# Sums of x split before the norms' copy, and the value projections' weight sums by adding DMAs, in a hybrid decoder trunk

## The chip, the cores and the metric

The kernel runs on one core of a Trainium2 chip. The metric is the device time of one execution in microseconds. The kernel before takes 791.1 us, the median of three runs (790.81 to 793.31). The engines are named as the profile names them: PE is TensorE (matmuls), PEld its loads of the stationary operand, DVE is VectorE, ACT ScalarE, POOL GpSimd, SP SyncE, which issues most DMAs. Each engine executes its own instructions in the order of the program and waits at an instruction until the semaphores it names are there.

## The reference

One layer of a decoder trunk for one sequence of 512 tokens, D = 1024, with 16 learned meta tokens in front (528 rows), all float32:

```python
u = rms_norm(h, norm_gain)                       # h: 16 meta rows, then x
proj = u @ w_in                                  # one combined projection, cut into
(rq, rk, rv, rg, gq, gk, gv, gg, glr, m_ret, m_gla) = jnp.split(proj, points, axis=-1)
o_ret = retention(rope(rq), rope(rk), rv)        # 4 heads: keys of 256, values of 512
o_ret = head_group_norm(o_ret) * silu(rg)
log_a = log_sigmoid(glr @ w_gate_up + b_gate) / 16
o_gla = gated_linear_attention(gq, gk, gv, log_a)  # 4 heads: keys of 128, values of 256
o_gla = head_rms_norm(o_gla) * silu(gg)
merged = sigmoid(m_ret) * (o_ret @ w_branch_ret) + sigmoid(m_gla) * (o_gla @ w_branch_gla)
out = rms_norm(h + merged @ w_out, final_norm_gain)[meta rows dropped]
```

## The kernel before, in words

PE works in fp32r. A float32 operand is split into a high part (a cast on ACT, `_h`) and a low part (a subtraction on DVE, `_l`), both at line 153, and a product takes three matmuls (high by high, high by low, low by high). A weight block of 128 partitions x 1024 elements (512 rows by 256 columns of w_in) is loaded raw by SP's queue into one of six buffers, and split into one of three buffers for each part.

The projections through w_in are done in groups of a 512-row by 512-column piece with two halves of tokens, two of columns and two of the depth (`quad`). A group is not done as eight products of blocks but as seven, in the manner of Strassen and Winograd: sums of x's blocks (S1 to S4, split once for the whole kernel into `fh`/`fl`) meet sums of weight blocks. The seven products come in the order 1, 2, 6, 7, 5, 4, 3, each 24 matmuls of 128x256 into one of the PSUM banks b, a, c. Product 1 takes the block w11, product 2 w21, product 6 w11 + x3 (added on DVE into w11), product 7 the sum x3, product 5 the sum x1, product 4 w21 + the new w11 (DVE), product 3 w22. The sums x3 and x1 come in one of two ways. With `adds` true, SP loads one block and POOL issues a second DMA that adds the other block to it in memory. With `adds` false, four blocks are loaded and DVE makes the two sums (lines 315 and 316). Before each product its weights are split, so ACT and DVE work one or two products ahead of PE. Results leave PSUM by copies (`_x`) and additions (`vs`, and its split vh, vl).

The groups come in this order: gv0, gq0 and gk0 (plain projections, `proj_a`), gg0, gqk1, gv1, gg1; then for each retention head h the group rqk, then rg, the gates mg or mr and the branch projection br of an earlier head, and rv; at the end the output projection wo. "Value groups" here are gv1 and rv0 to rv3; rv groups come directly before the next head's rqk.

The 16 meta tokens would make a poor moving operand, so their rows for keys and values are made by 32-column matmuls on the unsplit weights (`um` stationary, line 306), four row groups into one PSUM bank (`psm`, in the trace rv_pm or rqk_pm); the bank is then split (rvm_h, rvm_l) and its row groups are summed by two matmuls with a selection matrix (rvm_s, lines 446 and 447). In a value group before, the sixteen such matmuls are done ahead of product 1 from w11, w21, w12, w22; the split and the summing are deferred by a list, `late`, which is run out after product 5 (and after product 1).

The scheduler inside the framework places instructions by their dependences; the dense matmuls are pinned in the order of the program (`pin`, `order`), and `act` and `vec` chain instructions of the first part on ACT and DVE. `weave` steps a dense generator and a second chain of work in turn, and calls `tick` between steps.

At the start, x is loaded, its blocks' sums are made (u00, u01, u10, u11), gv0 runs on the plain blocks, the norms' reciprocal root is spread over the columns (PE's rb, copied to SBUF by ACT), and gq0 and gk0 follow; woven into them are the GLA forget gates (z, Abs, Exp and a correction at lines 654 to 664) and `sums()`, the split of the four sums of x, which gg0 is the first group to need.

Of the kernel before, what the change touches and what calls it, by code (L numbers as in the profile page):

```python
# [20 lines left out]
F32 = mybir.dt.float32  # L21
# [6 lines left out]
P = 128  # L28
D = 1024
T = 512  # L30
NM = 16
# [76 lines left out]
def hybrid_kernel(ctx: ExitStack, tc: tile.TileContext, I, out: bass.AP):  # L108
# [30 lines left out]
    rb = cp.tile([P, 2, HT], F32, name="rb")  # L139
    um = cp.tile([P, KD, 32], F32, name="um")  # L140
    sel = cp.tile([P, P], F32R, name="sel")
# [54 lines left out]
    def rstd_of(x, n, rows, name, eps=EPS):  # L196
        v = sp.tile([P, 1], F32, tag="rv", name=f"{name}_v")
        r = sp.tile([P, 1], F32, tag="rr", name=f"{name}_r")
        nc.vector.tensor_scalar(v[:rows], x, 1.0 / n, eps, op0=ALU.mult, op1=ALU.add)
        nc.gpsimd.tensor_tensor(r[:rows], v[:rows], mhalf[:rows], op=ALU.pow)  # L200
        return r
# [29 lines left out]
    def tick():  # L231

        pend[:] = [(n - 1, f) for n, f in pend]
        while pend and pend[0][0] <= 0:
            pend.pop(0)[1]()

    late = []
# [12 lines left out]

    def quad(cols, rows, name, evac, meta=None, adds=True):

# [25 lines left out]
        def product(i, form, w, ps, fresh):  # L278
            hi, lo = wsplit([P, 4, 256], f"{name}_{i}")
            split(hi, lo, w)  # L280
            for t in range(2):
                col = slice(t * P, (t + 1) * P)
                for kk in range(4):
                    u = [f[form][:, kk, col] if rows else f[form][:, kk, :256] for f in (fh, fl)]
                    v = [f[:, kk, :] if rows else f[:, kk, col] for f in (hi, lo)]
                    first = fresh and kk == t == 0
                    for j, (x1, x2) in enumerate(((0, 0), (0, 1), (1, 0))):
                        l, r = (u[x1], v[x2]) if rows else (v[x1], u[x2])
                        m = nc.tensor.matmul(ps[:, t, :], l, r, start=first and j == 0, stop=kk == 3 and j == 2,  # L289
                                             skip_group_check=not fresh or t == 1)  # L290
                        if t == kk == j == 0:
                            pin(m)
            order[:] = [m]
# [7 lines left out]
        if meta is not None:  # L301
            psm = (ppt if adds else pat)(f"{name}_pm")
            for n in range(1 if adds else 2):
                for kh in range(2):
                    for g in range(4):
                        nc.tensor.matmul(psm[32 * g:32 * g + 32, n * 256:(n + 1) * 256], um[:, 4 * kh + g, :],
                                         (w11, w21)[kh][:, g, :] if n == 0 else (w12, w22)[kh][:, g, :], start=n == 0 and kh == 0, stop=kh == 1,
                                         skip_group_check=n > 0)
        product(1, A11, w11, b, True)
# [16 lines left out]
        x = copy(c, 3)  # L326
        if meta is not None:
            late.append(lambda: meta(psm))
        yield
        product(5, S1, x1, b, False)  # L330
# [3 lines left out]
        product(4, A22, w21, c, False)  # L334
        evac(0, 1, c, y)
        yield
        product(3, S4, w22, b, False)
# [220 lines left out]
    for kh in range(2):  # L558
        for k in range(4):
            x = nc.scalar.activation(u[kh][:, k], u[kh][:, k], AF.Copy, scale=ng[:, 4 * kh + k:4 * kh + k + 1])  # L560
            if kh == 1:
                act(x)
        x = nc.vector.tensor_copy(um[:, 4 * kh:4 * kh + 4, :NM].rearrange("p k (h m) -> p k h m", h=2),
                                  u[kh][:, :, :, 256:HT])
        if kh == 1:
            vec(x)
    u00, u01, u10, u11 = u[0][:, :, 0], u[1][:, :, 0], u[0][:, :, 1], u[1][:, :, 1]
    vec(nc.vector.tensor_sub(u11, u11, u10))
# [42 lines left out]
    leave(2)  # L611
    leave(3)
    act(nc.scalar.copy(rb[:, :, :256], rbm.rearrange("p (h t) -> p h t", h=2)))
    act(nc.scalar.copy(rb[:, :, 256:], rbp[:, HT:HT + NM].rearrange("p (h m) -> p h m", h=2)))
    h, l = split(*parts["gq0", 1], loaded.pop(("gq0", 1)))
    act(h)
    vec(l)

    def sums():
        for i, x in ((S2, u00), (S3, u10), (S1, u11), (S4, u01)):  # L620
            h, l = split(fh[i][:, :, :HT], fl[i][:, :, :HT], x)
            after(h, ends["act"])
            after(l, ends["vec"])
            yield

# [69 lines left out]
    def gla_v(p):  # L695
        yield from quad((C_GV + p * 512, C_GV + p * 512 + 256), True, f"gv{p}", rows_into(gv[p]),
                        lambda psm: meta_v(psm, p), False)

# [5 lines left out]
    def gla_qk(p):  # L704
# [26 lines left out]
        if p:  # L731
            yield from quad((C_GK + p * 256, C_GQ + p * 256), False, f"gqk{p}", evac, meta)
            return
# [189 lines left out]
    next(gates)  # L923
    weave(gla_qk(0), turns(sums(), gates))
    for i in range(4):
# [42 lines left out]
    def ret_qk(h):  # L968

        q = rp.tile([P, 2, 2, 256], F32, tag="ql", name=f"q{h}")  # L970
        k = rp.tile([P, 2, 2, HT], F32, tag="kl", name=f"k{h}")
        R["raw", h] = q, k

        def evac(n, th, x, y):
            total(q[:, :, th] if n else k[:, :, th, :256], x, y)

        def meta(psm):
            nc.scalar.copy(k[:, :, :, 256:], meta_columns(psm, f"rkm{h}"))

        yield from quad((C_RK + h * 256, C_RQ + h * 256), False, f"rqk{h}", evac, meta)  # L980

# [24 lines left out]
    def ret_v(h):  # L1006
# [23 lines left out]

        yield from quad((C_RV + h * 512, C_RV + h * 512 + 256), True, f"rv{h}", evac, meta, False)

# [32 lines left out]
    def ret_attention(h):  # L1065
# [7 lines left out]
        def values(ib):  # L1073
            ps = pat(f"av{h}{ib}")
            for jb in range(ib + 1):
                o = SOFF[jb] + (ib - jb) * P
                mm3(ps, sh[:, o:o + P], sl[:, o:o + P], vh[:, jb, :], vl[:, jb, :], jb == 0, False)
            nc.tensor.matmul(ps, sm[:, ib * P:(ib + 1) * P], vm, start=False, stop=True)
            b6 = sp.tile([P, 6], F32, tag="b6", name=f"b6{h}{ib}")
            mv = sp.tile([P, 2], F32, tag="mv", name=f"mv{h}{ib}")  # L1080
            nc.vector.bn_stats(b6, ps)
            nc.vector.bn_aggr(mv, b6)
            r = rstd_of(mv[:, 1:2], 1.0, P, f"g{h}{ib}")
            nm = sp.tile([P, 1], F32, tag="nm", name=f"nm{h}{ib}")
            nc.vector.scalar_tensor_tensor(nm, mv[:, 0:1], -1.0, r, op0=ALU.mult, op1=ALU.mult)  # L1085
            on = tmp(f"on{h}{ib}")
            nc.scalar.activation(on, ps, AF.Identity, scale=r, bias=nm)  # L1087
            nc.vector.tensor_mul(sg[:, ib, :], on, sg[:, ib, :])
# [104 lines left out]
    def evac_out(half):  # L1193
        def f(t, ps, o=0, n=512):
# [10 lines left out]
            if half == 0 or o + n < 512:  # L1205
                return
            r = sp.tile([P, 1], F32, tag="rr", name=f"fr{t}")
            nc.gpsimd.tensor_tensor(r, v, mhalf, op=ALU.pow)
# [58 lines left out]
```

## Time and profile before

| what | value |
|---|---|
| median of three runs | 791.1 us (790.81 to 793.31) |
| the profiled execution | 791.0 us, its span 789.2 us |
| PE busy | 771.3 us, 98% of the span, 5407 matmuls |
| DVE, ACT, POOL busy | 570.7, 449.5, 139.8 us |
| DMA | 117.91 MB, HBM read 99.20 MB |

A row of a timeline reads: start in us, duration, engine, line, operation, output<-input, shapes, how many; in brackets, if the engine was idle before, how long and whose work ended that. In a table of windows each engine has its busy time and count, and after them come PE's granted clock, the share of the DMA engines and GB/s. The instructions of a group bear the names of their buffers without the number that tells them apart, so that `rv_h` is the high part of any product of any rv group.

### The profile page before, as it was taken

The page shows a single profiled execution, that of the slowest core. Times are in us where ns is not written, and L with a number is a line of the kernel's source. Part 1 is how long each engine was busy: PE and PEld are TensorE (multiplying, and loading weights), DVE is VectorE, ACT ScalarE, POOL GpSimd, SP SyncE. Part 2 cuts the span into 40 slices and gives each one's busy share as a digit, 9 for nine tenths or more (in the row PEclk, how much of TensorE's full clock was granted, in tenths as well). Part 3 has the DMA queues.
Part 4 walks back from the last instruction along what each step waited for, and adds up shares of the span by engine and source line. Part 5 has one row for each costly group of instructions (what it writes and reads, how often), then busy time and mean ns, then how long its engine had stood idle before and what let it go on. Part 6 is the DMA issues. An engine that isn't in the chain of part 4 may idle for free.

```text
span 789.2 us, 13635 instructions
## 1 busy us (share of the span) xinstructions
PE 771.3 (98%) x5407; PEld 699.3 (89%) x5407; DVE 570.7 (72%) x824; ACT 449.5 (57%) x743; POOL 139.8 (18%) x200
## 2 busy tenths in 40 slices
PE   8999999999999999999999999999999899999996
PEld 5788989999889899989989999989999898888785
DVE  5588688677654579778967687977686988576832
ACT  7697775677654456546646545645455655363422
POOL 2110220101312313100320100340111101333031
PEclk9999999999999999999999999999999999999999
DMA  9871703642148983833684562695475327799202
GB/s 284 261 185 39 171 12 98 150 144 81 67 129 207 242 185 108 187 107 108 183 240 137 112 156 108 161 246 131 123 153 122 108 81 215 121 306 304 94 2 106
DMA packets 94601, 117.91 MB, mean 149 GB/s; under 512 B 5957, under 2 KB 80581, under 8 KB 94281
## 3 DMA queue, kind: packets, MB, share of 16 engines
q1 hardware_dynamic: 74600, 85.58, 35.7%
q0 software_dynamic: 19936, 31.46, 20.5%
q8 instruction: 42, 0.69, 0.4%
q14 instruction: 23, 0.18, 0.1%
HBM read 99.20 MB, written 17.83 MB: 148 GB/s over the span
## 4 chain that ended last, share of the span: by engine, by line
PE 79%; DVE 8%; ACT 4%; DMA 4%; issue 3%; POOL 1%; POOLq 0%; SPq 0%; DVEq 0%; ACTq 0%
PE rv_b L289 6%; PE rg_b L289 5%; PE rqk_b L289 4%; PE mg_b L289 3%; PE rg_c L289 3%; PE br_p L192 3%; PE br_p L191 3%; PE br_p L188 3%; PE rv_c L289 2%; PE gg_b L289 2%; PE rqk_c L289 2%; PE bg_p L192 2%; PE bg_p L191 2%; PE bg_p L188 2%; PE wo_p L188 2%
## 5 line engine op out<-in xcount | busy, mean ns | idle before, releaser
L192 PE MATMUL br_p<-oh,br_l 128*128 128x512 f32 x128 | 50.6, 395 | 0.0
L191 PE MATMUL br_p<-ol,br_h 128*128 128x512 f32 x128 | 50.5, 395 | 0.0
L188 PE MATMUL br_p<-oh,br_h 128*128 128x512 f32 x128 | 50.5, 395 | 0.0
L153 ACT CAST rv_h<-rv_w 128x1024 fp32r<-128x1024 f32 x24 | 25.3, 1052 | 28.2 <-DVE rv_w L318 10.2
L1087 ACT ACTIVATE on<-av,nm,g_r 128x512 f32<-128x512 f32 x16 | 12.5, 778 | 48.7 <-DVE nm L1085 48.6
L885 POOL DMA_DIRECT2D kept<-mt x24 | 19.8, 825 | 109.7 <-ACT mt L1147 109.5
L153 DVE TENSOR_TENSOR rv_l<-rv_w,rv_h 128x1024 fp32r<-128x1024 f32 x24 | 29.3, 1222 | 8.8 <-ACT rv_h L153 8.8
L153 DVE TENSOR_TENSOR rg_l<-rg_w,rg_h 128x1024 fp32r<-128x1024 f32 x20 | 24.4, 1221 | 7.9 <-ACT rg_h L153 7.9
L192 PEld LDWEIGHTS br_p<-oh,br_l 128*128 128x128 f32 x128 | 24.0, 187 | 5.8
L191 PEld LDWEIGHTS br_p<-ol,br_h 128*128 128x128 f32 x128 | 24.0, 188 | 5.2
L188 PEld LDWEIGHTS br_p<-oh,br_h 128*128 128x128 f32 x128 | 24.0, 188 | 5.1
L153 DVE TENSOR_TENSOR rqk_l<-rqk_w,rqk_h 128x1024 fp32r<-128x1024 f32 x20 | 24.4, 1221 | 5.3 <-ACT rqk_h L153 5.3
L269 POOL DMA_DIRECT2D rqk_x<-in_w_in_dram x8 | 10.4, 1306 | 98.2 <-DVE vl L153 50.3
L188 PE MATMUL wo_p<-wo_h,mh 128*128 128x512 f32 (+1 forms) x72 | 26.6, 370 | 0.7 <-DVE mt L1152 0.7
L289 PE MATMUL rg_b<-rg_l,fh 128*128 128x256 f32 x96 | 27.0, 282 | 0.3 <-DVE rg_l L153 0.3
L153 ACT CAST rg_h<-rg_w 128x1024 fp32r<-128x1024 f32 x20 | 21.0, 1052 | 11.0 <-PE br_p L191 5.0
L289 PE MATMUL rqk_b<-fh,rqk_h 128*128 128x256 f32 x96 | 27.2, 284 | 0.0
L289 PE MATMUL rqk_b<-fh,rqk_l 128*128 128x256 f32 x96 | 27.1, 283 | 0.1
L289 PE MATMUL rqk_b<-fl,rqk_h 128*128 128x256 f32 x96 | 27.0, 282 | 0.0
L289 PE MATMUL rv_b<-rv_h,fl 128*128 128x256 f32 x96 | 27.0, 281 | 0.0
L289 PE MATMUL rv_b<-rv_l,fh 128*128 128x256 f32 x96 | 27.0, 281 | 0.0
L289 PE MATMUL rg_b<-rg_h,fh 128*128 128x256 f32 x96 | 27.0, 281 | 0.0
(645 smaller groups left out, 3168.5 us busy)
## 6 DMA issues: line engine op xcount, KB each, us to landing
rv_w<-in_w_in_dram SPq DMA_DIRECT2D x16, 512.0 KB, 4.1
br_w<-in_w_branch_ret_dram SPq DMA_DIRECT2D x16, 512.0 KB, 3.5
rqk_w<-in_w_in_dram SPq DMA_DIRECT2D x12, 512.0 KB, 4.9
rg_w<-in_w_in_dram SPq DMA_DIRECT2D x12, 512.0 KB, 4.3
kept<-mt POOLq DMA_DIRECT2D x24, 256.0 KB, 5.3
bg_w<-in_w_branch_gla_dram SPq DMA_DIRECT2D x8, 512.0 KB, 3.7
mr_w<-in_w_in_dram SPq DMA_DIRECT2D x8, 512.0 KB, 3.8
kept<-gb POOLq DMA_DIRECT2D x16, 256.0 KB, 3.8
```

The lines of the kernel that those rows point to most:

```text
L153: return nc.scalar.copy(hi, src), nc.vector.tensor_sub(lo, src, hi.bitcast(F32))
L188: m = nc.tensor.matmul(o, lh, rh, start=first, stop=False)
L191: nc.tensor.matmul(o, lh, rl, start=False, stop=False)
L192: m = nc.tensor.matmul(o, ll, rh, start=False, stop=last)
L269: nc.gpsimd.dma_start(t, block(0, 1), accum_op=ALU.add)
L289: m = nc.tensor.matmul(ps[:, t, :], l, r, start=first and j == 0, stop=kk == 3 and j == 2, skip_group_check=not fresh or t == 1)
L885: nc.gpsimd.dma_start(dst, t, **({} if first else {"accum_op": ALU.add}))
L1087: nc.scalar.activation(on, ps, AF.Identity, scale=r, bias=nm)
```

## The change

There are three parts. First, the split of the four sums of x no longer is a generator woven into gq0 and gk0; it stands in the chain of ACT and DVE ahead of the copies of rb. Second, the value groups take their weight sums x3 and x1 the way all other groups with `adds` do, by an SP load and an adding DMA of POOL; so the block w12 alone is no longer in memory. Third, the meta rows of the second 256 columns, which were made from w12 and w22, are therefore made from blocks that are there: x3 = w22 + w12 with the first half of the meta tokens after product 7, and w22 with a new third part of `um` (second half minus first half, one POOL subtraction) after product 4. The count of matmuls stays. So the split of the meta rows and their summing come after product 4; and `tick` runs the list `late`, so that in qk groups (`first`) they come right after product 7 is issued, and in value groups right after product 4. Four small tags get more buffers (not shown).

```diff
...
-    um = cp.tile([P, KD, 32], F32, name="um")
+    um = cp.tile([P, 3 * KD // 2, 32], F32, name="um")
...
         pend.pop(0)[1]()
+        run_late()
...
-    def quad(cols, rows, name, evac, meta=None, adds=True):
+    def quad(cols, rows, name, evac, meta=None, adds=True, first=False):
...
         if meta is not None:
-            psm = (ppt if adds else pat)(f"{name}_pm")
-            for n in range(1 if adds else 2):
-                for kh in range(2):
-                    for g in range(4):
-                        nc.tensor.matmul(psm[32 * g:32 * g + 32, n * 256:(n + 1) * 256], um[:, 4 * kh + g, :],
-                                         (w11, w21)[kh][:, g, :] if n == 0 else (w12, w22)[kh][:, g, :], start=n == 0 and kh == 0, stop=kh == 1,
-                                         skip_group_check=n > 0)
+            psm = ppt(f"{name}_pm")
+
+        def rows_of_meta(i, form, w):
+
+            n = i // 2 * 256
+            for g in range(4):
+                nc.tensor.matmul(psm[32 * g:32 * g + 32, n:n + 256], um[:, 4 * form + g, :], w[:, g, :],
+                                 start=i == 0, stop=i % 2 == 1, skip_group_check=i > 1)
+
+        if meta is not None:
+            rows_of_meta(0, 0, w11)
+            rows_of_meta(1, 1, w21)
         product(1, A11, w11, b, True)
         x = copy(b, 1)
         run_late()
...
         yield
         product(7, S3, x3, c, True)
         x = copy(c, 3)
-        if meta is not None:
+        if meta is not None and first:
             late.append(lambda: meta(psm))
+        elif meta is not None:
+            rows_of_meta(2, 0, x3)
         yield
         product(5, S1, x1, b, False)
         evac(1, 1, b, x)
...
         yield
         product(4, A22, w21, c, False)
         evac(0, 1, c, y)
+        if meta is not None and not first:
+            rows_of_meta(3, 2, w22)
+            late.append(lambda: meta(psm))
         yield
         product(3, S4, w22, b, False)
         evac(1, 0, b, None)
...
+    nc.gpsimd.tensor_sub(um[:, 8:, :NM], um[:, 4:8, :NM], um[:, :4, :NM])
...
     leave(2)
     leave(3)
+    for i, x in ((S2, u00), (S3, u10), (S1, u11), (S4, u01)):
+        qsplit(fh[i][:, :, :HT], fl[i][:, :, :HT], x)
     act(nc.scalar.copy(rb[:, :, :256], rbm.rearrange("p (h t) -> p h t", h=2)))
...
-    def sums():
-        for i, x in ((S2, u00), (S3, u10), (S1, u11), (S4, u01)):
-            h, l = split(fh[i][:, :, :HT], fl[i][:, :, :HT], x)
-            after(h, ends["act"])
-            after(l, ends["vec"])
-            yield
...
     def gla_v(p):
         yield from quad((C_GV + p * 512, C_GV + p * 512 + 256), True, f"gv{p}", rows_into(gv[p]),
-                        lambda psm: meta_v(psm, p), False)
+                        lambda psm: meta_v(psm, p))
...
-            yield from quad((C_GK + p * 256, C_GQ + p * 256), False, f"gqk{p}", evac, meta)
+            yield from quad((C_GK + p * 256, C_GQ + p * 256), False, f"gqk{p}", evac, meta, first=True)
...
-    weave(gla_qk(0), turns(sums(), gates))
+    weave(gla_qk(0), gates)
...
-        yield from quad((C_RK + h * 256, C_RQ + h * 256), False, f"rqk{h}", evac, meta)
+        yield from quad((C_RK + h * 256, C_RQ + h * 256), False, f"rqk{h}", evac, meta, first=True)
...
-        yield from quad((C_RV + h * 512, C_RV + h * 512 + 256), True, f"rv{h}", evac, meta, False)
+        yield from quad((C_RV + h * 512, C_RV + h * 512 + 256), True, f"rv{h}", evac, meta)
```

How the instructions stand on the engines now. On ACT in rv1, around the split of the meta rows (rvm_h) and of the weights of product 4 and 3 (rv_4_h, rv_3_h). Before:

```order
L153 CAST rvm_h<-rv_pm 128x512 [waits Activation_49]
L298 COPY rv_x_5119<-rv_c 128x512 [waits PE_49,Activation_49]
L153 CAST rv_4_h<-rv_w_4967 128x1024 [waits Activation_49]
L153 CAST rv_3_h<-rv_w_4969 128x1024 [waits DMAHW0_49,DVE_49,PE_49]
L1028 ACTIVATE vh_4964<-vs_5149 128x2x256 [waits DVE_49]
L1014 CAST vm_5160<-rvm_s 128x512 [waits PE_49]
L153 CAST rqk_1_h<-rqk_w_5227 128x1024 [waits DMAHW1_49,Activation_49]
```

With the change:

```order
L154 CAST rv_4_h<-rv_w_4970 128x1024 [waits Activation_49]
L300 COPY rv_x_5115<-rv_c 128x512 [waits PE_49,Activation_49]
L1036 ACTIVATE vh_4967<-vs_5149 128x2x256 [waits DVE_49]
L154 CAST rvm_h<-rv_pm 128x512 [waits PE_49,Activation_49]
L154 CAST vh_4967<-vs_5181 128x2x256 [waits DVE_49]
L154 CAST rv_3_h<-rv_w_4973 128x1024 [waits DMAHW3_49,Activation_49]
L1022 CAST vm_5196<-rvm_s 128x512 [waits PE_49]
L154 CAST rqk_1_h<-rqk_w_5231 128x1024 [waits DMAHW4_49,Activation_49]
```

The meta rows' split stood three instructions ahead of the split of product 3's weights with two others between; it stands two ahead now, and behind the evacuation of product 5 (vh from vs); one more vh, of product 4's result, stands between. Lines in the changed kernel are one to thirteen numbers higher for the same code.

On PE at the same place, before (the last matmul of product 5, rvm_s, and the first of product 4):

```order
L289 MATMUL rv_b<-rv_5_h,fl_88 128x256
L446 MATMUL rvm_s<-rvm_h,sel 128x512 [waits Activation_49]
L447 MATMUL rvm_s<-rvm_l,sel 128x512 [waits DVE_49]
L289 MATMUL rv_c<-rv_4_h,xh_81 128x256 [waits Activation_49]
L289 MATMUL rv_c<-rv_4_l,xh_81 128x256 [waits DVE_49]
```

With the change (the last matmul of product 4, what stands between, and the first two of product 3):

```order
L291 MATMUL rv_c<-rv_4_h,xl_83 128x256
L310 MATMUL rv_pm<-rv_w_4973,um 32x256 [waits DMAHW3_49]
L310 MATMUL rv_pm<-rv_w_4973,um 32x256 x3
L310 MATMUL rqk_pm<-rqk_w_5231,um 32x256 [waits DMAHW4_49,PE_49]
L310 MATMUL rqk_pm<-rqk_w_5231,um 32x256 x3
L310 MATMUL rqk_pm<-rqk_w_5232,um 32x256 [waits DMAHW7_49]
L458 MATMUL rvm_s<-rvm_h,sel 128x512 [waits Activation_49]
L310 MATMUL rqk_pm<-rqk_w_5232,um 32x256 x3
L459 MATMUL rvm_s<-rvm_l,sel 128x512 [waits DVE_49]
L291 MATMUL rv_b<-rv_3_h,fh_87 128x256 [waits Activation_49]
L291 MATMUL rv_b<-rv_3_l,fh_87 128x256 [waits DVE_49]
```

Four meta matmuls of rv1's w22, the first ones of the next group (rqk_pm) and the two rvm_s stand between product 4 and product 3; before, the two rvm_s stood between products 5 and 4, and the meta matmuls of the group ahead of product 1.

On ACT at the start: from the middle of the sums' splits to the first split of gk0 (gk_0_h), before (fh are the sums' high parts, gvm the meta rows of gv0, fg_e and fg_a the forget gates'):

```order
L153 CAST fh_85<-u_130 128x4x264
L153 CAST fh_86<-u_130 128x4x264
L533 ACTIVATE gvm_110<-gvm_s,rt 16x512 [waits PE_49,Pool_49]
L659 ACTIVATE fg_e_509<-z_507 128x512 [waits PE_49]
L659 ACTIVATE fg_e_517<-z_515 128x512 [waits PE_49]
L660 ACTIVATE fg_e_509<-fg_e_509 128x512 [waits Activation_49]
L660 ACTIVATE fg_e_517<-fg_e_517 128x512 [waits Activation_49]
L662 ACTIVATE fg_a<-fg_e_509,one 128x512 [waits Activation_49]
L662 ACTIVATE fg_a<-fg_e_517,one 128x512 [waits Activation_49]
L153 CAST fh_84<-u_131 128x4x264
L153 CAST fh_87<-u_131 128x4x264
L153 CAST gk_0_h<-gk_w_597 128x1024 [waits DMAHW0_49]
```

With the change the four fh stand ahead of the copy of rb. Here is the gate bias work (fg_b, fg_wz), and then the rows up to gk_0_h:

```order
L654 ACTIVATE fg_b<-fg_a 128x256 [waits DMAHW6_49,DVE_49,Pool_49]
L654 ACTIVATE fg_b<-fg_a 128x8
L545 ACTIVATE gvm_110<-gvm_s,rt 16x512 [waits PE_49,Pool_49]
L654 ACTIVATE fg_b<-fg_a 128x256 [waits DVE_49]
L654 ACTIVATE fg_b<-fg_a 128x8
L657 CAST fg_wz<-la 128x512 [waits DMAHW4_49,DMAHW5_49,DMAHW3_49,DMAHW6_49,DMAHW2_49,DMAHW7_49,DMAHW1_49,DMAHW0_49]
```

```order
L667 ACTIVATE fg_e_492<-z_490 128x512 [waits PE_49]
L667 ACTIVATE fg_e_500<-z_498 128x512 [waits PE_49]
L668 ACTIVATE fg_e_492<-fg_e_492 128x512 [waits Activation_49]
L668 ACTIVATE fg_e_500<-fg_e_500 128x512 [waits Activation_49]
L670 ACTIVATE fg_a<-fg_e_492,one 128x512 [waits Activation_49]
L670 ACTIVATE fg_a<-fg_e_500,one 128x512 [waits Activation_49]
L667 ACTIVATE fg_e_532<-z_530 128x512 [waits PE_49]
L667 ACTIVATE fg_e_540<-z_538 128x512 [waits PE_49]
L668 ACTIVATE fg_e_532<-fg_e_532 128x512 [waits Activation_49]
L668 ACTIVATE fg_e_540<-fg_e_540 128x512 [waits Activation_49]
L154 CAST gk_0_h<-gk_w_624 128x1024 [waits DMAHW0_49]
```

The evacuation of gvm stands between the two halves of fg_b; before, it stood behind both and behind fg_wz. Before gk_0_h there were the gates' Abs, Exp and correction of two z blocks; now there are those and the Abs and Exp of two more.

More of the change, by code (lines that the diff above doesn't have):

```diff
@@ L196, in rstd_of @@
     def rstd_of(x, n, rows, name, eps=EPS):
-        v = sp.tile([P, 1], F32, tag="rv", name=f"{name}_v")
-        r = sp.tile([P, 1], F32, tag="rr", name=f"{name}_r")
+        v = sp.tile([P, 1], F32, tag="rv", name=f"{name}_v", bufs=4)
+        r = sp.tile([P, 1], F32, tag="rr", name=f"{name}_r", bufs=4)
         nc.vector.tensor_scalar(v[:rows], x, 1.0 / n, eps, op0=ALU.mult, op1=ALU.add)
@@ L285, in product @@
                     v = [f[:, kk, :] if rows else f[:, kk, col] for f in (hi, lo)]
-                    first = fresh and kk == t == 0
+                    clear = fresh and kk == t == 0
                     for j, (x1, x2) in enumerate(((0, 0), (0, 1), (1, 0))):
                         l, r = (u[x1], v[x2]) if rows else (v[x1], u[x2])
-                        m = nc.tensor.matmul(ps[:, t, :], l, r, start=first and j == 0, stop=kk == 3 and j == 2,
+                        m = nc.tensor.matmul(ps[:, t, :], l, r, start=clear and j == 0, stop=kk == 3 and j == 2,
                                              skip_group_check=not fresh or t == 1)
@@ L1078, in values @@
             nc.tensor.matmul(ps, sm[:, ib * P:(ib + 1) * P], vm, start=False, stop=True)
-            b6 = sp.tile([P, 6], F32, tag="b6", name=f"b6{h}{ib}")
-            mv = sp.tile([P, 2], F32, tag="mv", name=f"mv{h}{ib}")
+            b6 = sp.tile([P, 6], F32, tag="b6", name=f"b6{h}{ib}", bufs=3)
+            mv = sp.tile([P, 2], F32, tag="mv", name=f"mv{h}{ib}", bufs=3)
             nc.vector.bn_stats(b6, ps)
@@ L1083, in values @@
             r = rstd_of(mv[:, 1:2], 1.0, P, f"g{h}{ib}")
-            nm = sp.tile([P, 1], F32, tag="nm", name=f"nm{h}{ib}")
+            nm = sp.tile([P, 1], F32, tag="nm", name=f"nm{h}{ib}", bufs=3)
             nc.vector.scalar_tensor_tensor(nm, mv[:, 0:1], -1.0, r, op0=ALU.mult, op1=ALU.mult)
@@ L1206, in f @@
                 return
-            r = sp.tile([P, 1], F32, tag="rr", name=f"fr{t}")
+            r = sp.tile([P, 1], F32, tag="rr", name=f"fr{t}", bufs=4)
             nc.gpsimd.tensor_tensor(r, v, mhalf, op=ALU.pow)
```

## The prediction

> **What bounds the kernel now.** I read the page's shares first, then the waits of PE, then the stretch around its longest wait.
>
> ```profile
> span 789.2 us, 13635 instructions
> PE 771.3 (98%) x5407; PEld 699.3 (89%) x5407; DVE 570.7 (72%) x824; ACT 449.5 (57%) x743; POOL 139.8 (18%) x200
> PE 79%; DVE 8%; ACT 4%; DMA 4%; issue 3%; POOL 1%; POOLq 0%; SPq 0%; DVEq 0%; ACTq 0%
> ```
>
> TensorE's own instruction stream is the bound: 771.3 of 789.2 us. The change keeps the number of matmuls, so DVE's and POOL's totals count for nothing by themselves; only what makes PE wait longer or shorter counts, and what its clock does. PE's waits:
>
> ```profile
> PE gk_p L371 <- DVE gk_l L153: 1.8, 1, 1.8
> PE rg_a L289 <- DVE rg_l L153: 1.4, 1, 1.4
> PE gg_b L289 <- DVE gg_l L153: 0.6, 1, 0.6
> PE gg_b L289 <- ACT gg_h L153: 0.5, 1, 0.5
> PE gm L799 <- POOL gto L772: 0.4, 1, 0.4
> ```
>
> The columns are total us, times, longest. All are waits for the split of a weight block (a cast on ACT, then a subtraction on DVE), and no row names a value group (gv1, rv0 to rv3). The waits that the first edit can touch are gk's 1.8 and gg0's 0.6 + 0.5 + 0.4. The first costs more than its length:
>
> ```profile
> 52.62 0.39 PE L371 MATMUL gk_p<-xh,gk_l 128*128 128x264 f32 x1 [1.78 <-DVE gk_l L153]
> 57.06 0.28 PE L371 MATMUL gk_p<-xh,gk_h 128*128 128x264 f32 x1
> 52.60:55.00 2.40, 2.38 (x12) 2.38 (x13) 2.40 (x4) 2.40 (x5) 0.00 (x0) 0.59 0.53 124
> 613.00:616.00 3.00, 2.07 (x17) 2.07 (x18) 3.00 (x4) 1.40 (x3) 0.00 (x0) 1.00 0.00 0
> ```
>
> In the windows the number before the last two is PE's granted clock: 0.59 after the 1.78 us wait, while the 1.4 us wait of rg_a, whose stretch is the last row, left it at 1.00. Between the two quoted matmuls lie 23 steps in 4.44 us; at the usual 0.119 us (24 matmuls of a product in 2.85 us) they take 2.74, so the low clock cost **1.7 us**.
>
> **The value groups (the large term).** What moves is a queue position on ACT. One product of rv1 before, with its neighbours:
>
> ```profile
> 446.55 0.59 ACT L153 CAST rvm_h<-rv_pm 128x512 fp32r<-128x512 f32 x1
> 451.75 1.05 ACT L153 CAST rv_h<-rv_w 128x1024 fp32r<-128x1024 f32 x1 [1.25 <-PE rv_b L289]
> 451.56 0.39 PE L446 MATMUL rvm_s<-rvm_h,sel 128*128 128x512 f32 x1
> 451.79 0.39 PE L447 MATMUL rvm_s<-rvm_l,sel 128*128 128x512 f32 x1
> 452.01 0.28 PE L289 MATMUL rv_c<-rv_h,xh 128*128 128x256 f32 x1
> 452.84 1.23 DVE L153 TENSOR_TENSOR rv_l<-rv_w,rv_h 128x1024 fp32r<-128x1024 f32 x1 [0.39 <-ACT rv_h L153]
> 454.76 0.28 PE L289 MATMUL rv_b<-rv_h,fh 128*128 128x256 f32 x1
> 457.70 1.07 PE L306 MATMUL rqk_pm<-rqk_w,um 128*32 128x256 f32 x16
> ```
>
> Product 4 runs on PE from 452.01 to 454.76. In that time the weights of product 3 are split (cast 451.75, subtraction to 454.07), so product 3 starts with no idle time at 454.76. The meta split (rvm_h) was done 5 us earlier. In the changed kernel the meta rows need four more matmuls after product 4, on w22; rvm_h waits for them, and the cast of product 3's weights stands behind rvm_h on ACT, its subtraction behind rvm_l on DVE. ACT and DVE take their instructions in order, so a split that ran under product 4 starts only after it. The durations:
>
> ```profile
> L153 ACT CAST rvm_h<-rv_pm x4: 592/594/595, 321.5 to 644.0; 128x512 fp32r<-128x512 f32 x4
> L153 DVE TENSOR_TENSOR rvm_l<-rv_pm,rvm_h x4: 691/691/692, 322.1 to 644.6; 128x512 fp32r<-128x512 f32 x4
> L153 ACT CAST rv_h<-rv_w x24: 1049/1052/1057, 304.9 to 651.4; 128x1024 fp32r<-128x1024 f32 x24
> L153 DVE TENSOR_TENSOR rv_l<-rv_w,rv_h x24: 1207/1224/1227, 306.6 to 652.5; 128x1024 fp32r<-128x1024 f32 x24
> L153 ACT CAST vh<-vs x8: 612/621/625, 319.4 to 657.7; 128x512 fp32r<-128x512 f32 x8
> 435.35 1.93 PE L306 MATMUL rv_pm<-rv_w,um 128*32 128x256 f32 x32
> ```
>
> The last row is 16 meta matmuls in 1.93 us, 0.12 each. Let T be the end of product 4's stream in rv1 or rv2. Four meta matmuls: 0.48, their result some 0.3 later, T+0.8. rvm_h starts at T+0.87 and ends at T+1.46; the cast vh of product 4's result follows (T+1.97, casts overlap by about 0.1); then product 3's cast to T+2.93 and its subtraction from T+2.96 to T+4.19. Product 3's second matmul needs that: T+4.23. PE has to do meanwhile: 0.48, eight meta matmuls of the next group (0.96), the two rvm_s (0.23 apart, 0.46), and one matmul of product 3 (0.12), together 2.02. **Stall 2.2 us** in each of rv1 and rv2. The work in it was PE's before as well, so only the stall is new.
>
> The others differ in what PE has for cover. rv0 also has score matmuls there, six of 256 columns (0.12 each, 0.70) and four of 512 (0.23 each as the rvm_s, 0.92), which leaves 0.6. rv3 has those scores but no meta matmuls of a next group (0.48 + 0.46 + 0.70 + 0.92 + 0.12 = 2.68 of work) and so 1.55 to wait, and DVE multiplies one of the scores ahead of rv_3_l, some 0.2 more: 1.75. gv1 has eight narrow matmuls of the scan there (0.12 to 0.17 each, 1.15) in place of rqk's 0.96, and ACT one more copy of results in front: 2.3. Sum 2 × 2.2 + 0.6 + 1.75 + 2.3 = **+9.05**. From below, if rvm_h and vh come early enough to cost the split nothing (0.48 + 0.5), each stall shrinks by 1.0, but not below zero: 1.2 + 1.2 + 0 + 0.75 + 1.3 = +4.45. From above, each is 0.4 longer: +11.
>
> **Their adding DMAs.** Each value group drops two DVE adds; x3 and x1 come as one load on SP and one adding DMA on POOL.
>
> ```profile
> L269 POOL DMA_DIRECT2D rqk_x<-in_w_in_dram x8 | 10.4, 1306 | 98.2 <-DVE vl L153 50.3
> rv_w<-in_w_in_dram SPq DMA_DIRECT2D x16, 512.0 KB, 4.1
> ```
>
> Ten more on POOL at 1.3 us is 13 us on an engine busy for 139.8; a load lands in 4.1 and the adding one in about as much again, on buffers given free some 10 us ahead of their product. No PE wait: 0. The ten removed adds saved no PE wait either, since no value group had one. If the cover is gone, product 6 waits up to about 4 us in a group (a rival). The one tensor_sub on POOL for the meta rows lies under the norms: 0.
>
> The sooner rkm and gkm splits (run_late in tick) stand a product earlier, but in qk groups the meta rows are complete before product 1, so they wait for nothing: 0, at worst 1 us in one group.
>
> **The start.** The four casts and subtractions move into idle time:
>
> ```profile
> 34.93 0.59 ACT L613 COPY rb<-rb 128x512 f32<-128x512 f32 x1 [4.29 <-PE rb L606]
> 36.57 1.23 DVE L153 TENSOR_TENSOR gq_l<-gq_w,gq_h 128x1024 fp32r<-128x1024 f32 x1 [5.62 <-ACT gq_h L153]
> 41.00 2.05 ACT L153 CAST fh<-u 128x1056 fp32r<-128x1056 f32 x2
> 42.10 2.43 DVE L153 TENSOR_TENSOR fl<-u,fh 128x1056 fp32r<-128x1056 f32 x2 [0.29 <-ACT fh L153]
> 43.24 0.68 ACT L533 ACTIVATE gvm<-gvm_s,rt 16x512 f32<-16x512 f32 x1 [0.19 <-PE gvm_s L447]
> 43.34 0.62 PE L654 MATMUL z<-fg_wz,fg_b 128*128 128x512 f32 x2
> 43.83 1.04 ACT L659 ACTIVATE fg_e<-z 128x512 f32<-128x512 f32 x2
> 45.82 1.32 ACT L662 ACTIVATE fg_a<-fg_e,one 128x512 f32<-128x512 f32 x2
> 47.05 2.03 ACT L153 CAST fh<-u 128x1056 fp32r<-128x1056 f32 x2
> 48.99 1.04 ACT L153 CAST gk_h<-gk_w 128x1024 fp32r<-128x1024 f32 x1
> ```
>
> ACT has 4.29 idle for 4.1 of casts, DVE 5.62 for 4.9, so the move itself is hidden. But the gates' instructions move with it. In the new order gvm<-gvm_s, which waits for PE until 43.24, stands ahead of half of the gate bias work, so the z matmuls come 19 matmuls later (43.34 + 2.3 = 45.6), and gk_0_h now stands behind the Abs and Exp of four z, not two. From 45.9: two Abs (L659) 1.04, two Exp about 1.1, two L662 1.32, then two Abs and two Exp 2.2: gk_0_h from 51.5 to 52.55, gk_0_l to 53.8, PE 53.85 against 52.62. **+1.2 to +1.4**, with the low clock after it as before. DVE and ACT then have 5 us less to do, so gg0's waits of 0.6 + 0.5 + 0.4 mostly go: **-1.0**. Together +0.4; from below -4.9 (gk's 1.8, the 1.7 of clock and gg0's 1.5 all gone, if ACT reaches gk_h at 47), from above +2.
>
> **rg3.** Here DVE's order also moves: the norm statistics of ret head 2's last block come behind a split of rqk3.
>
> ```profile
> 601.38 0.69 DVE L1081 BATCH_NORM_STATS2 b<-av 128x6 f32<-128x512 f32 x1
> 612.65 1.22 DVE L153 TENSOR_TENSOR rg_l<-rg_w,rg_h 128x1024 fp32r<-128x1024 f32 x1
> ```
>
> They start one split (1.2 us) later; what hangs on them (the turned output, then rg's split, which PE already waits 1.4 for) is that much later: **+1.1**, between 0 and 2.
>
> **Clock.** Three of the new stalls (gv1, rv1, rv2) are longer than the 1.78 that lowered the clock, though pieces of matmul work lie between their parts; 1.4 did not lower it. I take half a fall in all, 0.5 × 1.7 = +0.85; from above four falls, +6.8. [...]
>
> **Sum**: 9.05 + 0.4 + 1.1 + 0.85 = 11.4. The profiled execution took 791.0 (span 789.2 and 1.8 around it), the median of the runs is 791.1, so they are the same: 791.0 + 11.4 = **802.4 us**.
>
> **Rivals.** (A) *The value groups don't stall and the start gains.* If product 3's split is ready in time (say, ACT's wait ends with the first meta matmul) and gk_h comes early: 791.0 - 4.9 = 786. For it: the idle 4.29 and 5.62 are real. Against: one fixed queue on ACT. Chance 0.05. (B) *Start gains, stalls small.* The bounds -4.9 and +4.45 cancel: 790.5, no change. Chance 0.07. (C) *The clock falls at each long stall*: four times 1.7 more than nothing, 791.0 + 10.55 + 6.8 = 808.4. For it: 1.78 did it once; against: matmuls inside the stalls, and 1.4 did not. It decides where idle within a few us passes about 1.6. Chance 0.15. (D) *The adding DMAs are late*: product 6 waits up to 4 us in two of the five groups, 810. It decides if a buffer comes free less than 8 us ahead of its product; against it, POOL's 18%. Chance 0.08. (E) *The change of order costs only half*: one small cast hides in each stall, 797. Chance 0.15. The forecast has 0.5.
>
> Of this kernel's runs the highest is 0.3% above the median, so 0.3% (2.4 us) is what I call no change. Faster holds A and a little of B, 0.06; the same the rest of B and a little of E, 0.07; slower the others, 0.87. The range 795 to 809 leaves out A, B and part of D.
>
> **What would show it.** Right: PE rows of waits in gv1, rv1, rv2 and rv3 at the first matmuls of product 3 (rv_b <- rv_l), 1.7 to 2.3 us each, about 0.6 in rv0; rvm_h directly after product 4, the cast of product 3 after it; gk_p's wait 3 us in all and gg0's gone; PE's busy time the same but for the clock. Wrong: no wait in rv groups, or rv_h of product 3 starting during product 4; gk_p's wait under 1 us; waits of product 6 or 5 on a DMA; or granted clocks below 1 in the value groups, which would decide for C.

## The result, and the profile after

The changed kernel takes **803.3 us** (median of four runs, 802.71 to 805.79) against 791.1 for the kernel before (four runs by now, 790.81 to 793.31): slower by a ratio of 1.0154, 95% interval 1.0126 to 1.0182. The forecast was 802.4. The profiled execution took 803.4 us, and its page begins and its chain ends so:

```profile
span 801.6 us, 13676 instructions
PE 776.7 (97%) x5407; PEld 697.9 (87%) x5407; DVE 560.1 (70%) x814; ACT 448.8 (56%) x743; POOL 163.4 (20%) x211
PE 60%; DVE 10%; DMA 9%; issue 7%; ACT 6%; POOL 2%; POOLq 0%; DVEq 0%; ACTq 0%; SPq 0%
```

PE does the same 5407 matmuls. DVE has ten instructions and 10.6 us less, and it buys nothing. The chain now runs through PE for 60% of the span instead of 79%: there are more places where PE's next matmul hangs on another engine. PE's waits (total us, times, longest):

```profile
PE rv_b L291 <- DVE rv_l L154: 2.7, 4, 0.9
PE gm L807 <- POOL gto L780: 1.2, 1, 1.2
PE z L662 <- DVE la L672: 1.2, 1, 1.2
PE rqk_b L291 <- ACT rqk_x L300: 1.0, 1, 1.0
PE ot L442 <- DVE sg L1096: 0.9, 1, 0.9
PE gk_p L383 <- ACT gk_h L154: 0.6, 1, 0.6
PE gk_p L383 <- DVE gk_l L154: 0.5, 1, 0.5
```

The first row is new: PE waits for a weight's low part in rv groups four times, three of them at product 3 (rv1 and rv2 0.9, rv3 0.5) and one at product 6 of rv0 (0.5, told below). In rv1 the timeline shows why (PE, ACT and DVE in order of time):

```profile
462.36 0.64 PE L310 MATMUL rv_pm<-rv_w,um 128*32 128x256 f32 x8
463.12 0.59 ACT L154 CAST rvm_h<-rv_pm 128x512 fp32r<-128x512 f32 x1 [1.96 <-PE rv_pm L310]
463.61 0.62 ACT L154 CAST vh<-vs 128x512 fp32r<-128x512 f32 x1
464.12 1.05 ACT L154 CAST rv_h<-rv_w 128x1024 fp32r<-128x1024 f32 x1
465.21 1.23 DVE L154 TENSOR_TENSOR rv_l<-rv_w,rv_h 128x1024 fp32r<-128x1024 f32 x1 [0.18 <-ACT rv_h L154]
466.49 0.39 PE L291 MATMUL rv_b<-rv_l,fh 128*128 128x256 f32 x1 [0.87 <-DVE rv_l L154]
```

ACT sits idle for 1.96 us with the cast of product 3's weights ready to run, because rvm_h stands ahead of it and waits for the four meta matmuls after product 4. Product 4's stream ended at T = 462.27, so the second matmul of product 3 came at T+4.22; T+4.23 was forecast. By the forecast's count PE had 2.02 us of work meanwhile, so 2.2 were lost, of which the table of waits shows 0.87. The rest hides behind rows that count as busy: a matmul's row (0.28, and 0.39 after a wait) is longer than the 0.12 from one start to the next, so it covers the beginning of a short wait. The rows of PEld in the same stretch are shorter and show four more gaps, of 0.41, 0.24, 0.41 and 0.28. It would also be why PE's busy time rose by 5.4 us with no matmul added.

Where the 12.4 us of the span came from, worked out from the first matmul of each group in the two timelines (the eight meta matmuls that moved from in front of a value group into it, 0.87 us, are set right):

| stretch | forecast | measured |
|---|---|---|
| start to the end of gg0 | +0.4 | +0.9 |
| gqk1 to the start of rqk0 (gv1) | +2.3 | +1.8 |
| rqk0 | 0 | +1.1 |
| rg0, rv0 | +0.6 | +3.3 (0.7 of it in rg0) |
| rqk1 | 0 | +1.0 |
| rv1, rqk2 | +2.2 | +2.35 |
| rv2, rqk3 | +2.2 | +1.9 |
| rg3 | +1.1 | -2.1 |
| rv3 | +1.75 | +2.6 |
| falls of the clock at the new waits | +0.85 | 0 |
| the rest | 0 | -0.5 |

The sum was right within a microsecond, and luck has a part in that. rv0 with rg0 came out 2.7 dearer than forecast, rqk0 1.1, rqk1 1.0 and rv3 0.85; rg3 came out 3.2 cheaper and the clock's 0.85 did not come. These misses nearly cancelled.

### The profile page after: what moved, and what is told of

The parts are those of the page before. It is cut to its first block, busy times and chain, and to the rows that moved or that the text cites. A ratio compares the mean times of both kernels' runs of the same rounds, so it can differ in the third digit from the quotient of the medians.

```text
span 801.6 us, 13676 instructions
## 1 busy us (share of the span) xinstructions
PE 776.7 (97%) x5407; PEld 697.9 (87%) x5407; DVE 560.1 (70%) x814; ACT 448.8 (56%) x743; POOL 163.4 (20%) x211
## 4 chain that ended last, share of the span: by engine, by line
PE 60%; DVE 10%; DMA 9%; issue 7%; ACT 6%; POOL 2%; POOLq 0%; DVEq 0%; ACTq 0%; SPq 0%
PE rv_b L291 5%; PE rqk_b L291 4%; PE rg_b L291 4%; PE mg_b L291 3%; PE rv_c L291 3%; PE br_p L192 3%; PE br_p L193 3%; PE br_p L189 3%; DMA rv_x<-in_w_in_dram 3%; DMA kept<-gb 2%; PE gg_b L291 2%; PE rqk_c L291 2%; PE wo_p L189 2%; PE wo_p L192 2%; PE wo_p L193 2%
## 5 line engine op out<-in xcount | busy, mean ns | idle before, releaser
L154 ACT CAST rv_h<-rv_w 128x1024 fp32r<-128x1024 f32 x20 | 21.0, 1051 | 18.0 <-DVE rv_w L325 10.5
L154 ACT CAST rg_h<-rg_w 128x1024 fp32r<-128x1024 f32 x20 | 21.0, 1050 | 12.2 <-PE br_p L192 5.0
L291 PE MATMUL rv_b<-rv_h,fh 128*128 128x256 f32 x96 | 27.4, 285 | 0.3 <-ACT rv_x L300 0.3
L154 DVE TENSOR_TENSOR rv_l<-rv_w,rv_h 128x1024 fp32r<-128x1024 f32 x20 | 24.4, 1221 | 4.3 <-ACT rv_h L154 4.3
L291 PE MATMUL rg_b<-rg_h,fl 128*128 128x256 f32 x96 | 27.0, 281 | 0.0
```

The source lines that it names most:

```text
L154: return nc.scalar.copy(hi, src), nc.vector.tensor_sub(lo, src, hi.bitcast(F32))
L291: m = nc.tensor.matmul(ps[:, t, :], l, r, start=clear and j == 0, stop=kk == 3 and j == 2, skip_group_check=not fresh or t == 1)
```

## The experiments

The theory: the time is lost by the position of the meta rows' split in ACT's and DVE's queues, not by the adding DMAs, and the move of the sums of x costs about 1 us. The rivals: the adding DMAs; the sums' move as a hidden gain; the deferred list in `tick`.

**The meta split after product 3.**

```diff
...
             rows_of_meta(3, 2, w22)
-            late.append(lambda: meta(psm))
         yield
         product(3, S4, w22, b, False)
         evac(1, 0, b, None)
+        if meta is not None and not first:
+            late.append(lambda: meta(psm))
...
```

> The changed kernel (803.3 us), with one thing undone: in value groups the split and summing of the meta rows are emitted after product 3 instead of ahead of its split; the four late meta matmuls stay after product 4, the adding DMAs stay. Theory (ACT's and DVE's queue position is what costs): the waits at product 3 go, 2.35 in rv1, 2.5 in rv2, 2.6 in rv3, about 2 in rv0 and 1.8 in gv1, so 803.3 - 11 = 792 to 794 us. Rival (the adding DMAs, or the extra meta matmuls between products, cost the time): 800 or more.

Measured: 796.4 us, 1.0040 of the kernel before (1.0027 to 1.0053). That is 6.9 us back, not 11, between the two expectations. By its timeline the waits at product 3 of gv1, rv1 and rv2 went (these groups now cost 0.1, 0.6 and 0.6). rv0 (with rg0) still costs 2.1 and rv3 1.5, and rg3, which had gained 2.1 us in the changed kernel, gave most of that back:

```profile
PE rg_a L291 <- DVE rg_l L154: 1.9, 1, 1.9
```

**All meta rows after product 7, their split after product 5.** This is where the kernel before had the split; the adding DMAs stay.

```diff
...
         elif meta is not None:
             rows_of_meta(2, 0, x3)
+            rows_of_meta(3, 2, w22)
...
         evac(1, 1, b, x)
+        if meta is not None and not first:
+            late.append(lambda: meta(psm))
...
-        if meta is not None and not first:
-            rows_of_meta(3, 2, w22)
-            late.append(lambda: meta(psm))
...
```

> The changed kernel with both late groups of meta matmuls (on x3 and on w22) after product 7, and their split and summing after product 5, where the kernel before had them; adding DMAs stay. Theory: as in the kernel before, the split of product 3 runs under product 4: 792 to 794 us, with what is left over the kernel before (about 1 to 2 us) being rv0's wait for its adding DMA and the first groups. Rival (adding DMAs): 800 or more. Rival (w22 arrives too late for its meta matmuls after product 7): a wait of PE on a DMA there, 796 or more.

Measured: 793.5 us, ratio 1.0012 (1.0002 to 1.0023), as the theory had it. **9.8 of the 12.2 us are the position of four matmuls and of the split behind them.** (In these runs the kernel before took 791.95, 0.8 more than in the first ones, so the 9.8 is good to about 1 us.) gv1, rv1 and rv2 cost 0.4, 0.3 and 0.3; rv0 (with rg0) still 1.8 and rv3 0.9. So w22 is there in time, and the adding DMAs are no large cost, but not nothing in rv0 and rv3.

**What holds rv0's adding DMAs.** In the changed kernel POOL and DVE show it:

```profile
304.50 5.82 POOL L998 CAST km<-kl 128x32 fp32r<-128x32 f32 x1 [1.52 <-DVE kl L154]
310.26 2.59 POOL L271 DMA_DIRECT2D rv_x<-in_w_in_dram  x2
319.24 1.22 DVE L325 TENSOR_TENSOR rv_w<-rv_w,rv_x 128x1024 f32<-128x1024 f32 x1 [3.11 <-DMA rv_x<-in_w_in_dram]
322.98 0.39 PE L291 MATMUL rv_b<-rv_l,fh 128*128 128x256 f32 x1 [0.46 <-DVE rv_l L154]
```

POOL issues the two adding DMAs only at 310.26, behind a small copy of the retention head's meta keys (km) that took 5.82 us. The sum of product 6 then waits for the DMA, and PE for its split; product 6's second matmul comes 1.2 us late. The slow copy is not new, the kernel before has it too, but there no DMA stands behind it on POOL for another 17 us:

```profile
299.73 5.22 POOL L990 CAST km<-kl 128x32 fp32r<-128x32 f32 x1 [2.66 <-DVE kl L153]
```

Only rv0 and rv3 share their stretch with those copies. So the km copies alone were moved, from POOL to ACT, on top of the version just told of:

```diff
...
-            nc.gpsimd.tensor_copy(km[...], (kh if r < 3 else kl)[:, :, :, 256:HT].bitcast(F32))
+            nc.scalar.copy(km[...], (kh if r < 3 else kl)[:, :, :, 256:HT].bitcast(F32))
...
```

> The earlier kernel with all meta rows after product 7 (793.5 us) with one thing moved: the four small copies of a retention head's meta keys (km) from POOL to ACT. Theory: in rv0 and rv3 POOL's two adding DMAs stand behind those copies, which ended at 310.3 and 638.1 in the changed kernel; without them they are issued some 4 to 7 us sooner and the waits at product 6 go, 1.8 in rv0 and 0.9 in rv3: 793.5 - 2.7 = 790.8 us. Rival (the adding DMAs are late by the transfer itself, or ACT's four more instructions cost as much): 793 to 794.

Measured: 790.95 us, ratio 0.9989 (0.9979 to 0.9998); expected 790.8. The copy takes 0.2 us on ACT, and the first adding DMA goes out at 302.33, for 310.26 in the changed kernel and 308.36 in the version that this one starts from:

```profile
301.67 0.22 ACT L998 CAST km<-kl 128x32 fp32r<-128x32 f32 x1
302.33 1.29 POOL L271 DMA_DIRECT2D rv_x<-in_w_in_dram  x1 [11.35 <-DVE rg_l L154]
```

rv0 (with rg0) went from +1.8 to +0.3 and rv3 from +0.9 to +0.3, together 2.1 of the 2.7. PE's wait at mr_b, behind rv3, grew by 0.4, and about 1 us came in other stretches that this edit does not touch, so the agreement of the totals is better than that of the parts.

**The sums' move alone**, on the kernel before:

```diff
...
+    for i, x in ((S2, u00), (S3, u10), (S1, u11), (S4, u01)):
+        qsplit(fh[i][:, :, :HT], fl[i][:, :, :HT], x)
     act(nc.scalar.copy(rb[:, :, :256], rbm.rearrange("p (h t) -> p h t", h=2)))
...
-    weave(gla_qk(0), turns(sums(), gates))
+    weave(gla_qk(0), gates)
...
```

> The kernel before (791.1 us) with the first edit alone: the splits of x's sums ahead of the copies of rb, the gates woven without them. Theory: PE waits at the z matmuls and at gk_0, about 1 us lost by the start of gqk1, no fall of the clock: 791.1 + 0.9 = 792.0 us. Rival (the move is a gain that the value groups hid): 787.

Measured: 792.6 us beside 791.95 for the kernel before in the same runs, ratio 1.0006 (0.9997 to 1.0016): no change that can be told, and no hidden gain. The timeline repeats the changed kernel's start, with gk's first matmul 2.9 us later than before.

**The sums' move with the gates' old pace.**

```diff
...
-    weave(gla_qk(0), gates)
+    weave(gla_qk(0), turns(blank(), gates))      # blank: four steps that do nothing
...
-        nc.scalar.activation(gvm[p], ps[:NM], AF.Copy, scale=rt[:NM, NTB:])
+        m = nc.scalar.activation(gvm[p], ps[:NM], AF.Copy, scale=rt[:NM, NTB:])
+        if p == 0:
+            act(m)
...
```

> As the previous one (the kernel before with the sums' splits moved), but the gates keep the pace they had (a step only after every second step of gq0 and gk0), and the evacuation of gvm is chained behind the gate bias work, where it stood before. Theory: gk_0's cast then follows two z blocks and starts near 47 us; gk's wait (1.78), the low clock behind it (1.7) and gg0's waits (1.1 to 1.5) go: 791.1 - 4.9 = 786 us. Rival (those waits are replaced by others in gg0, or the low clock comes from elsewhere): 789 to 791.

Measured: 791.6 us, ratio 1.0001 (0.9988 to 1.0013). The expectation of 786 fell. The same wait is there:

```profile
49.01 1.04 ACT L153 CAST gk_h<-gk_w 128x1024 fp32r<-128x1024 f32 x1
51.13 0.68 DVE L708 TENSOR_TENSOR gq<-gq_p,rb 128x512 f32<-128x512 f32 x1
51.72 1.21 DVE L153 TENSOR_TENSOR gk_l<-gk_w,gk_h 128x1024 fp32r<-128x1024 f32 x1
52.99 0.39 PE L371 MATMUL gk_p<-xh,gk_l 128*128 128x264 f32 x1 [1.83 <-DVE gk_l L153]
```

ACT's cast came at 49.0, not 47, since the z matmuls stand 18 matmuls later on PE than in the kernel before; and it wouldn't have helped, since gk_l stands on DVE behind four corrections of the gates and a copy of gq. The wait was DVE's order, which neither the sums nor ACT decide.

**gk0's first split ahead of the gates' z blocks**, added to that:

```diff
...
+        load_a(C_GK, 0, "gk0")
+        parts["gk0", 0] = wsplit([P, 4, 256], "gk0_0")
+        qsplit(*parts["gk0", 0], loaded["gk0", 0])
         for b in range(5):
             ps = pat(f"z{b}")
...
```

> The kernel before with the sums' splits moved, the gates at their old pace, and in addition the first split of gk0 emitted ahead of the gates' z blocks, so that its subtraction no longer stands behind the gates' corrections on DVE. Theory: gk's wait (1.8) and the fall of the clock behind it (1.7) go: 791.6 - 3.5 = 788.1 us, granted clock 1.00 from 40 to 60 us. Rival (a wait in gg0 takes their place): 791.

Measured: 788.15 us, ratio 0.9961 (0.9946 to 0.9975); expected 788.1. The wait at gk_p is gone, and gg0 starts 3.15 us earlier than in the kernel before. Whether gk0's split would do this without the move of the sums was not run. The profiled run shows what is late next: the wait of mr_b grew from 0.8, and the clock fell there instead (windows: busy time and count of PE, PEld, DVE, ACT, POOL, then granted clock, DMA share, GB/s):

```profile
PE mr_b L289 <- DVE mr_l L153: 1.7, 1, 1.7
694.00:696.00 2.00, 0.35 (x3) 0.14 (x2) 2.00 (x3) 0.00 (x0) 0.79 (x1) 1.00 1.07 336
696.00:700.00 4.00, 3.91 (x20) 3.91 (x21) 3.85 (x7) 1.26 (x3) 1.60 (x3) 0.57 1.08 251
```

**Without the deferred list in `tick`**: the changed kernel, with an own call ahead of product 3's split, and qk groups as before.

```diff
...
         while pend and pend[0][0] <= 0:
             pend.pop(0)[1]()
-        run_late()
...
         yield
+        run_late()
         product(3, S4, w22, b, False)
...
```

> The changed kernel (803.3 us) with the run of the deferred list taken out of tick; value groups keep their own at the same place (ahead of product 3's split), qk groups split their meta rows after product 5 again. The prediction gave this edit 0: 803.3 us. Rival (it costs the new waits of rqk0 and rqk1, 1.0 each): 801.3. Second rival (it is what freed rg3 of its 2.1 us of waits, by reordering DVE there): 805.

Measured: 802.4 us (801.53 to 803.31), too near to 803.3 to tell. The trace shows two effects that cancel. Without it rqk1's 1.0 us of waiting goes, and rg3's 2.1 us come back:

```profile
PE rg_a L290 <- DVE rg_l L154: 1.4, 1, 1.4
PE rg_b L290 <- DVE rg_l L154: 0.9, 1, 0.9
```

In this version, as in the kernel before, a split of rqk3 stands on DVE directly ahead of rg3's first split; with the edit of `tick` it stands ahead of the norm's statistics, and rg3's splits move up. The extra buffers of the norms' small tiles, which are a part of the change too, are in this version, so they alone don't give the gain. The edit of `tick` isn't the whole cause, though: the version with the split after product 3 has it, with the same order on DVE from rg3's first split to its second, and waits 1.9 at rg_a all the same. There DVE had stood idle in rqk3 for a norm's small POOL instruction (g_r), which came behind the issue of an adding DMA at 595.10:

```profile
597.04 0.16 DVE L1094 SCALAR_TENSOR_TENSOR nm<-mv,g_r 128x1 f32<-128x1 f32 x1 [2.53 <-POOL g_r L201]
```

In the changed kernel the same wait is 0.75. rg3's second split starts 33.9 us after rqk3's first matmul with that wait, and 31.8 us after it in the changed kernel. That this idle time is why is read from the rows; no run separated it.

**The repairs together**: meta rows after product 7, km on ACT, gates' pace, gvm and gk0 as above, on the changed kernel.

> The changed kernel with its three repairs together: meta rows after product 7, km copies on ACT, gates at their old pace with gk0's first split ahead of them. Theory: the terms add up, 790.8 - 0.6 (start's shift) - 2 = 788 us, a little faster than the kernel before, with rg3's 2.1 us gained and rqk0's 1 us of waiting for a DMA of the branch sums left. Rival (they don't add up, DMA waits take over): 791 to 793.

Measured: **787.5 us**, ratio 0.9948 (0.9932 to 0.9964) to the kernel before. It is faster than both kernels by more than the measurement's spread. The terms added up in the total, but not each in its place: in the profiled execution rg0 costs 1.2 us, with a wait for its split on DVE, where the version with km on ACT had lost nothing. Its largest waits:

```profile
PE wo_p L189 <- DVE mt L1169: 1.2, 2, 0.9
PE ge L770 <- ACT lah L154: 1.1, 1, 1.1
PE mr_b L291 <- DVE mr_l L154: 1.1, 1, 1.1
PE rqk_b L291 <- ACT rqk_x L300: 1.0, 1, 1.0
```

The last of these appears in nearly all versions, 0.3 to 1.3 us. In the changed kernel ACT stood for 6.7 us ahead of it, until an adding DMA of the branch sums (kept<-gb) had landed. What makes that DMA late was not tried.

## Why the prediction was right, and where not

**The value groups** were right in place, mechanism and size: a cast that ran under product 4 stood behind a cast that waits for product 4. rv1 was forecast at 2.2 and measured at 2.5, rv2 2.2 and 2.5 (their rows of the table hold -0.1 of rqk2 and -0.6 of rqk3), gv1 2.3 and 1.8. Undoing the position alone returned 9.8 us, about 8.8 of it in the table's stretches of these groups (1.4, 1.5, 2.1, 2.1 and 1.7 in those of gv1 and rv0 to rv3); the term was 9.05. The bounds, +4.45 and +11, held it. In rv0 itself the position cost 1.0 for a forecast of 0.6. The waits that the profile names at product 3 are shorter than the 1.7 to 2.3 us that the forecast wanted to see there (0.9, 0.9 and 0.5), for the reason told at rv1.

**Their adding DMAs, "No PE wait: 0"**, failed for rv0: one of the forecast's own signs of being wrong, a wait of product 6 that goes back to a DMA, is there. Of the 2.7 us that rg0 and rv0 cost beyond the forecast, 1.2 are this wait, 0.7 stand in rg0, at a wait for its split on DVE, and the rest is product 3's and smaller pieces. The step looked at POOL's 18% and at buffers given free 10 us ahead. It did not look at which instruction stands ahead of the DMA on POOL: an in-order queue is judged by the instruction in front (here the km copy of 5.82 us). It also let the adding transfer land in about as long as a load, 4.1 us; such transfers took longer in the kernel before already (first row), and in the changed kernel rv's own did (second row, median 8.4 us):

```profile
rqk_x<-in_w_in_dram POOLq DMA_DIRECT2D x8, 512.0 KB, 7.2
rv_x<-in_w_in_dram POOLq DMA_DIRECT2D x8, 512.0 KB, 8.4
```

The rival D had the right wait (product 6) with the wrong cause (a buffer) and too large a price (4 us for 1.2).

**The sooner rkm split, "0, at worst 1 us"**: rqk1 shows +1.0 (PE's wait `ot <- sg`, 0.9) and rg3 -2.1, and both go without the edit of `tick`. The step counted the moved instructions' own waits; it did not allow for DVE's other instructions changing places. The **rg3** term (+1.1) saw the statistics move behind a split, which they did, but not that rg's own split moved forward. **rqk0** (+1.1, the wait `rqk_b <- rqk_x`) was in no term, and its cause is open.

**The start** was right in its mechanism on ACT, with gvm and four z blocks ahead of gk0's split; here ACT, DVE and PE:

```profile
43.65 0.68 ACT L545 ACTIVATE gvm<-gvm_s,rt 16x512 f32<-16x512 f32 x1 [4.61 <-PE gvm_s L459]
46.29 1.16 PE L662 MATMUL z<-fg_wz,fg_b 128*128 128x512 f32 x4 [0.43 <-DVE fg_wz L658]
52.03 1.05 ACT L154 CAST gk_h<-gk_w 128x1024 fp32r<-128x1024 f32 x1
53.11 1.23 DVE L154 TENSOR_TENSOR gk_l<-gk_w,gk_h 128x1024 fp32r<-128x1024 f32 x1
54.40 0.39 PE L383 MATMUL gk_p<-xh,gk_l 128*128 128x264 f32 x1 [0.52 <-DVE gk_l L154]
```

The forecast had z at 45.6, gk_0_h at 51.5 and PE at 53.85, each 0.5 to 0.7 early. The 3 us of waiting that it put at gk_p came as 1.2 at a later z matmul, which it had not seen, and 0.6 and 0.5 at gk_p. The net +0.4 measured +0.9: the 1.0 that gg0's waits were to give back failed, since they make 2.1 now for 1.5 before. One of them grew, gm <- gto from 0.4 to 1.2; it waits for a copy on POOL and not, as the forecast says of all the rows, for a split.

**The clock, +0.85**: nothing of it came. No new stall lowered it (the granted clock stays at 1.00 through the value groups), and the fall at gk_p that was expected to stay was absent from this profile. What such a fall costs was also wrong, as the last section shows. Rival C has nothing left. Rival A's mechanism, a gain of the start, came only with gk0's split moved as well; the sums' move alone shows no gain.

## What to carry to other kernels

Before an instruction is moved later, read what stands behind it on its own engine: a 0.6 us cast that waits for the end of a product holds the split of the next one, and the price is the whole chain from there (cast, cast, subtraction) less what the consumer has left to do. Judge an in-order engine by the instruction ahead of the one that matters (5.82 us of copy ahead of rv0's adding DMAs), not by its share of busy time (20% for that POOL). When a scheduler orders the rest, expect one or two microseconds of either sign at places that the edit never names (here +1.0 in rqk1 and -2.1 in rg3), and look at several waits before crediting one of them.

## What the runs showed of the hardware

**The clock's fall is not fixed by the wait.** The changed kernel and the version with the split after product 3 have the same waits at z and gk_p (1.2, 0.6, 0.5 within 3 us), and yet in the same stretch (the rows as above; the changed kernel first):

```profile
55.00:57.00 2.00, 2.00 (x19) 2.00 (x18) 2.00 (x4) 2.00 (x4) 0.00 (x0) 1.00 0.69 199
```

```profile
55.00:57.00 2.00, 2.00 (x12) 2.00 (x12) 2.00 (x5) 2.00 (x5) 0.00 (x0) 0.57 0.57 138
```

Of the six profiles with this start two show the fall. It delayed gg0 by 1.5 us, and by the start of gqk1 nothing of it was left: gg0's wait gm <- gto is 0.4 us in the profile with the fall and 1.2 in that without, so 0.8 of the 1.5 was paid by that wait. The length of the waits doesn't sort the cases either. The clock fell after single waits of 1.78 us at gk_p (to 0.59, the kernel before) and 1.7 at mr_b (to 0.57, the version with gk0's first split ahead), and after the three that make 2.3 together (to 0.57); behind the same three it stayed at 1.00 in the changed kernel. A longer single wait didn't lower it, the 1.94 us at rg_a in the version with the split after product 3, so rival C's 1.6 us separates nothing here. What else decides it, no run shows. This is the row of the stretch right behind the 1.94 us:

```profile
620.00:622.00 2.00, 2.00 (x19) 2.00 (x18) 2.00 (x4) 0.64 (x1) 0.00 (x0) 1.00 0.03 8
```

**A copy of 128x32 elements for 7.2 us.** POOL's km copies take 0.2 to 1.5 us in the other places, but one takes 5.8 in rg0 and one 7.2 in rg3 (it is one of the three in the first row):

```profile
630.71 7.49 POOL L998 CAST km<-kh 128x32 fp32r<-128x32 f32 x3 [16.52 <-ACT kh L154]
637.74 0.69 DVE L687 TENSOR_TENSOR sg<-rg_b,rg_x 128x512 f32<-128x512 f32 x1
310.17 0.68 DVE L687 TENSOR_TENSOR sg<-rg_b,rg_x 128x512 f32<-128x512 f32 x1
```

Both times DVE ran instructions with two SBUF operands back to back (busy 5.80 of 5.80 us from 304.50, 7.50 of 7.50 from 630.70), and the copy ended within 0.2 us of the start of DVE's first instruction that reads one operand from PSUM (the two DVE rows; the copies ended at 637.9 and 310.3). In the kernel before it is the same, a copy that ended at 304.95 and the PSUM row at 304.82. That DVE's instructions hold the copy up is the author's reading of these three places, and not shown: the runs moved the copies off POOL (0.22 us for one on ACT) and did not separate this cause from others, and in rg3 of the kernel before a copy of km took 1.07 us (from 622.92) while DVE ran such instructions without a gap too (busy 5.30 of 5.30 us from 619.20).
